# Halved roundings and squares, value tiles and group A's norm through projection banks, transposed sums, and a new first transfer order in a hybrid encoder layer

## The chip, the cores and the metric

The kernel runs on one core of one Trainium2 chip. The metric is the device time of one execution in microseconds; the time before is the median of three runs, 1087.44 us (1087.1 to 1087.69). Durations of single instructions come from one execution that the hardware profiler recorded.

The engines are called by their short names: PE is the matrix engine (PEld its weight loads), DVE the vector engine, ACT the scalar engine, POOL the general engine and SP the engine that issues most transfers. PE writes its results to eight banks of 128 x 512 floats (PSUM); DVE and ACT read them there.

## The reference, cut to what matters

One layer: an RMS norm feeds one combined projection, whose columns are split between window attention with grouped queries (group A) and neighbourhood attention on a 16 x 64 grid (group B). Each group's output gets its own RMS norm, both go through one output projection, and a gated MLP with a width-3 convolution follows. All of it is float32, 1024 tokens, model width 1024, MLP width 2816.

```python
def rmsnorm(x, g):
    y = x * lax.rsqrt(jnp.mean(x * x, axis=-1, keepdims=True) + EPS)
    return y * g

hn = rmsnorm(h, norm_mix[l])
qa, ka, va, qb, kb, vb = jnp.split(hn @ w_in[l], splits, axis=-1)
o_a = window_gqa_sink(partial_rope(qa), partial_rope(ka), va, sink[l])   # |i-j| <= 128, 8 heads, 2 kv heads
o_b = neighbourhood_attention(qb, kb, vb, rpb[l])                        # 8 x 16 window, 8 heads
mix = concatenate([rmsnorm(o_a, norm_a[l]), rmsnorm(o_b, norm_b[l])])
h = h + mix @ w_out[l]
hn = rmsnorm(h, norm_ffn[l])
h = h + (silu(conv3(hn @ w_gate[l]) + conv_b) * (hn @ w_up[l])) @ w_down[l]
return rmsnorm(h, norm_final)
```

## The kernel before

Everything is held transposed: 128 features in the partitions, 1024 tokens in the columns, so x is eight tiles of 128 x 1024. A float32 product is made of three products of rounded parts: each operand is split into a rounded high part (ACT) and the remainder (DVE), and the block `hi*hi + hi*lo + lo*hi` runs as three matmuls of 512 columns (L168 to L170, later L883 to L885). The MLP products and the down projection use sums and differences of tiles, seven products in place of eight.

**PE's order is the program's order.** `manual_schedule` pins PE; the order of the other engines is made ahead of the run from the program's order, each instruction's priority (`high_priority(offset)` lifts it) and the time at which its operands are expected. Each engine then runs its list in order.

**The head.** `load_x`, `load_first_w` issue the first transfers in a fixed order over the SP and ACT queues: x tiles by halves or whole, and the first three weight tiles in slices of the reduction dimension (`steps`). `split_x` and `split_first_w` round what has landed, in a pinned order; six accumulating products use all of it. `add_square` adds up the squares for the first norm. A transfer takes one of a few completion counters; when all are in use, the next one waits on its queue for an earlier transfer to land.

**The norms.** A sum over the features is a sum over partitions. `inverse_narrow` makes it on PE: each 128-column block of the squares is the weight, a column of ones (1/1024) the moving operand, giving 128 tokens x 1 (L199); ACT takes the square root (L202) and DVE the reciprocal (L203). `widen` turns the four columns back into a 128 x 512 row by transposing a broadcast (L210). It is called for the first norm (`vs1`), group A (`narrow_a`, `wide_a`), group B (`vb2`), the FFN norm (twice) and the final norm (half 1, then half 0 by quarters).

**Attention with a filler.** From about 60 to 380 us, PE alternates attention steps with one block at a time of the remaining projections (`rest`, jobs `Project(3)` to `Project(17)`, then `OutA(0)` to `OutA(7)`). Numbers (job, block) in `aux` say where group A's norm is placed between blocks. PSUM has four tags with two banks each: `pj` for projections, `s` for scores, `pt` for transposed probabilities, `o` for attention outputs. An attention step makes scores in `s`, DVE adds the bias and finds the maximum (L366), ACT the exponential (L370), POOL scales (L374), PE transposes into `pt` (L406 in group A, L479 in B), ACT and DVE round that (`ph` L379, `pl` L380), and PE multiplies with the values (L411, L412 and L490, L491).

After a projection, `settle` calls `post` a few blocks into the next job. For a value tile `split_v` transposes it in two halves of four 128-column blocks (L297), each into a `pt` bank, from which ACT and DVE make the rounded value and its remainder (L301, L302). For queries and keys `split_pair` or `split_qk` round 1024 columns (ACT, then DVE at L274) and send four transfers. `done` tells attention which tiles are there; `squares`, `square_b` make the squares for the norms of groups A and B, 1024 columns at a time, `normed_a` (L726) multiplies group A's output by its norm.

**The tail.** The last product of the down projection is done for half 0 of the tokens by quarters of 256 columns, two output tiles (j = 2, 3) each, 11 blocks of three matmuls per tile and quarter. `leave_quarter` adds the residual (L1283) and squares (L1328). `finish` widens the norm into two banks: DVE multiplies six tiles from one (L1309), ACT copies the other (L1303) for POOL, which multiplies the two tiles in `APART` (L1307); each tile is then stored.

Of the kernel before, what the change touches and what calls it, by code (L numbers as in the profile page):

```python
# [20 lines left out]
KT = D // 128  # L21
# [32 lines left out]
def hybrid_layer(tc, xT, w_in, w_out, w_gate, w_up, w_down, small, sink, rpb, consts, rope, out):  # L54
    nc = tc.nc
    with ExitStack() as ctx:
# [127 lines left out]
        def squares(tiles, engine):  # L184
            acc = None
            for t in tiles:
                s2 = tmp("sq")
                nc.scalar.activation(s2, t, AF.Square)
                if acc is not None:
                    engine.tensor_tensor(s2, s2, acc, op=ALU.add)  # L190
                acc = s2
            return acc

        def inverse_narrow(sqs, dim, tag, n=4):

            ps = bank("ss", tag)
            for i, sq in enumerate(sqs):
                for c in range(n):
                    nc.tensor.matmul(ps[:, c:c + 1], sq[:, c * 128:(c + 1) * 128], ones[:, 0:1], start=c == 0 and i == 0,  # L199
                                     stop=i == len(sqs) - 1, skip_group_check=True)  # L200
            v = cpool.tile([128, 4], F32, name="v4", tag="v4", bufs=4)
            nc.scalar.activation(v[:, 0:n], ps[:, 0:n], AF.Sqrt, bias=eps, scale=float(D) / dim)  # L202
            nc.vector.reciprocal(v[:, 0:n], v[:, 0:n])  # L203
            return v

# [35 lines left out]
        def split_pair(t):  # L241

            a, b = big("q", "op", F32R), big("q", "op", F32R)
            nc.scalar.activation(a, t, AF.Copy, scale=-HD ** -0.5)
            lo = t[:, :].bitcast(F32R)
            nc.vector.scalar_tensor_tensor(lo, t, -HD ** -0.5, f32(a[:, :]), op0=ALU.mult, op1=ALU.subtract)
# [22 lines left out]
        def split_qk(t):  # L269

            a, b, q = big("ka", "op", F32R), big("kb", "op", F32R), big("q", "op", F32R)
            by = cst[:, K_SCALE:K_SCALE + 1]
            nc.scalar.activation(a, t, AF.Copy, scale=by)
            nc.vector.scalar_tensor_tensor(b, t, by, f32(a[:, :]), op0=ALU.mult, op1=ALU.subtract)  # L274
# [13 lines left out]
            nc.sync.dma_start(f32(a[o:o + 64, :]), f32(b[e:e + 64, :]))  # L288
            return a, b

        def split_v(t, halves):

            v = [big("v", "op", F32R) for _ in halves]
            for g in range(2):
                ps = bank("vt", "pt")
                for c in range(4):
                    nc.tensor.transpose(ps[:, c * 128:(c + 1) * 128], t[:, (4 * g + c) * 128:(4 * g + c + 1) * 128], ident)  # L297
                for i, e in enumerate(halves):
                    src = ps[:, :].rearrange("p (c w) -> p c w", w=128)[:, :, e * 64:e * 64 + 64]
                    dst = v[i][:, :].rearrange("p (c w) -> p c w", w=128)[:, 4 * g:4 * g + 4]  # L300
                    mark["value"] = nc.scalar.activation(dst[:, :, 0:64], src, AF.Copy)  # L301
                    nc.vector.tensor_tensor(dst[:, :, 64:128], src, f32(dst[:, :, 0:64]), op=ALU.subtract)  # L302
# [208 lines left out]


        done = set()
        mg, h1, norm = [None] * 8, [None] * KT, {}

        class Project:
            def __init__(self, m):
# [28 lines left out]

            def post(self):
                post(self.m, self.t)
                done.add(self.m)

        class OutA:
            def __init__(self, d):
# [56 lines left out]
            split_first_w(m, steps[1])  # L609
        for h in range(2):  # L610
            split_x(1, tsl(h))
        for m in range(3):
            split_first_w(m, steps[2])
        acc = add_square(xts[0], None)
        for k in range(2, KT):
            split_x(k)
            if k == 3:
                for m in range(3):
                    split_first_w(m, steps[3])
# [99 lines left out]
        def wide_a():  # L719
            live["op"] += 1  # L720
            norm["a"] = big("rstda", "op")
            for h in range(2):
                nc.scalar.activation(norm["a"][:, tsl(h)], widen(norm["v"][h], "pt"), AF.Copy)

        def normed_a(i):
            return lambda: nc.vector.scalar_tensor_tensor(  # L726
                mix[i], mix[i], col(C_NA + i), norm["a"], op0=ALU.mult, op1=ALU.mult)
# [53 lines left out]
        def square_b(u):  # L781

            if u == 40:
                sums["b"] = big("sqb", "op")
                nc.scalar.activation(sums["b"], mix[4], AF.Square)
            s2 = tmp("sq")
            nc.scalar.activation(s2, mix[5 if u == 40 else 6], AF.Square)
            nc.vector.tensor_tensor(sums["b"], sums["b"], s2, op=ALU.add)

        pend = None  # L790
        for i, item in enumerate(q_until(1, 4 + AHEAD)):
# [506 lines left out]

        def finish(h, v, cols=whole, split=False):
            n = (cols.stop - cols.start) // 128  # L1300
            wide, again = widen(v, "pt", n), widen(v, "pt", n)
            copy = half("wide")
            nc.scalar.activation(copy[:, cols], again[:, 0:128 * n], AF.Copy)  # L1303
            for i, d in enumerate([d for d in range(KT) if d not in APART] + list(APART)):
                x = at_res(d, h, cols)
                if d in APART:
                    nc.gpsimd.tensor_tensor(x, x, copy[:, cols], op=ALU.mult)  # L1307
                else:
                    nc.vector.scalar_tensor_tensor(x, x, col(C_NFIN + d), wide[:, 0:128 * n], op0=ALU.mult, op1=ALU.mult)  # L1309
                (nc.scalar if split and i % 2 else nc.sync).dma_start(out[d, :, h * HALF + cols.start:h * HALF + cols.stop], x)  # L1310
# [12 lines left out]
        def leave_quarter(j, ps, cols):  # L1323
# [50 lines left out]
        for k, cols in enumerate(quarters):  # L1374
            for j in (2, 3):
                ps = banks[6, j]
                for c, (f, n) in enumerate(PARTS):
# [108 lines left out]
```

## Time and profile before

| | |
|---|---|
| time, median of three runs | 1087.44 us (1087.1 to 1087.69) |
| time of the profiled execution | 1088.62 us |
| its span, first to last instruction | 1086.8 us |
| PE busy | 1070.2 us (98%), 5144 matmuls |
| DVE busy | 860.1 us (79%), 1570 instructions |
| ACT busy | 554.5 us (51%), 1047 instructions |
| POOL busy | 105.0 us (10%) |
| moved by transfers | 144.94 MB, 133 GB/s on average |
| mean granted PE clock | 0.997 |

The profile groups instructions by the line of the program that issued them (L168), the engine, and the tiles written and read (`pj<-xgh,whi`). In the timeline a row is: start, length, engine, line, operation, out<-in, count, and in brackets how long the engine stood idle before it and what ended that. In the table of waits a row is: who waited for whom, microseconds in total, how often, the longest. Matmuls overlap in the pipeline, so a row's length is not what PE pays for it; that is the distance from one start to the next.

### The profile page before, as it was taken

What the parts mean: (1) busy time and instruction counts of PE and PEld (TensorE: products, weight loads), DVE (VectorE), ACT (ScalarE), POOL (GpSimd) and SP (SyncE); (2) the same over time, 40 slices, a digit from 0 to 9 for tenths busy, and PEclk for the clock granted to TensorE, in tenths of its full rate; (3) what the DMA queues carried; (4) which work ended last, traced back from release to release, by engine and by line L of the source; (5) the groups of instructions that cost most, each with busy time, mean ns of one, the idle gap of its engine ahead of it and who ended that gap; (6) DMA issues with size and microseconds to landing.
All of it is one profiled execution on the core that took longest, in us unless ns stands there. A gap on an engine that the chain in (4) does not pass through costs nothing.

```text
span 1086.8 us, 14983 instructions
## 1 busy us (share of the span) xinstructions
PE 1070.2 (98%) x5144; PEld 895.0 (82%) x5144; DVE 860.1 (79%) x1570; ACT 554.5 (51%) x1047; POOL 105.0 (10%) x188
## 2 busy tenths in 40 slices
PE   8999999999999999999999999999999999999997
PEld 7888888888888888887788888888888888888887
DVE  6789787667788688899998877877887867897764
ACT  7457676556676545545434334342433645444451
POOL 0223332222232100000000000000000000000001
PEclk9999999999999999999999999999999999999998
DMA  8223022232225147214342222323322788867644
GB/s 275 73 73 88 30 68 59 78 77 78 78 68 161 65 137 249 88 39 157 134 146 107 107 107 97 120 95 111 111 88 97 244 297 295 272 214 241 227 129 155
DMA packets 69084, 144.94 MB, mean 133 GB/s; under 512 B 8208, under 2 KB 19600, under 8 KB 69008
## 3 DMA queue, kind: packets, MB, share of 16 engines
q1 hardware_dynamic: 58784, 118.43, 34.6%
q10 hardware_dynamic: 10224, 25.56, 6.2%
q8 instruction: 40, 0.66, 0.3%
q14 instruction: 36, 0.29, 0.1%
HBM read 103.58 MB, written 28.57 MB: 122 GB/s over the span
## 4 chain that ended last, share of the span: by engine, by line
PE 88%; DVE 8%; ACT 2%; DMA 1%; issue 1%; SPq 0%; POOL 0%; DVEq 0%; ACTq 0%; POOLq 0%
PE pj L168 7%; PE pj L169 7%; PE pj L170 7%; PE dn L883 6%; PE dn L885 6%; PE dn L884 6%; PE z L885 5%; PE z L884 5%; PE z L883 5%; PE s L344 3%; PE x L883 3%; PE x L884 3%; PE x L885 3%; PE y L885 3%; PE y L884 3%; PE y L883 3%
## 5 line engine op out<-in xcount | busy, mean ns | idle before, releaser
L872 ACT ACTIVATE whi<-ws 128x512 fp32r<-128x512 f32 (+1 forms) x100 | 60.3, 623 | 127.8 <-DVE ws L990 80.5
L883 PE MATMUL dn<-xd,whi 128*128 128x512 f32 (+1 forms) x330 | 124.1, 376 | 0.0
L885 PE MATMUL dn<-xd,wlo 128*128 128x512 f32 (+1 forms) x330 | 123.7, 375 | 0.0
L884 PE MATMUL dn<-xd,whi 128*128 128x512 f32 (+1 forms) x330 | 123.7, 375 | 0.0
L168 PE MATMUL pj<-xgh,whi 128*128 128x512 f32 x248 | 104.4, 421 | 1.0 <-ACT xgh L584 1.0
L885 PE MATMUL z<-hg,wlo 128*128 128x512 f32 x264 | 103.0, 390 | 0.7 <-DVE wlo L873 0.7
L883 PE MATMUL z<-hg,whi 128*128 128x512 f32 x264 | 102.9, 390 | 0.0
L884 PE MATMUL z<-hg,whi 128*128 128x512 f32 x264 | 102.7, 389 | 0.0
L370 ACT ACTIVATE p<-p,nm 128x385 f32<-128x385 f32 (+3 forms) x128 | 75.1, 587 | 50.4 <-DVE nm L366 49.3
L169 PE MATMUL pj<-xgl,whi 128*128 128x512 f32 x248 | 97.5, 393 | 0.9 <-DVE xgl L585 0.8
L170 PE MATMUL pj<-xgh,wlo 128*128 128x512 f32 x248 | 97.6, 394 | 0.0
L374 POOL TENSOR_SCALAR p<-p,sm 128x384 f32<-128x384 f32 (+1 forms) x128 | 74.9, 598 | 219.3 <-DVE sm L372 204.7
L873 DVE TENSOR_TENSOR wlo<-raw,whi 128x512 fp32r<-128x512 f32 (+1 forms) x102 | 66.4, 671 | 26.6 <-ACT whi L872 26.4
L872 ACT ACTIVATE whi<-raw 128x512 fp32r<-128x512 f32 (+1 forms) x102 | 60.6, 612 | 45.2 <-DMA raw<-in_w_down_dram 20.0
L873 DVE TENSOR_TENSOR wlo<-ws,whi 128x512 fp32r<-128x512 f32 (+1 forms) x100 | 66.9, 681 | 21.0 <-ACT whi L872 20.8
L380 DVE TENSOR_TENSOR pl<-pt,ph 128x384 fp32r<-128x384 f32 (+2 forms) x108 | 63.3, 589 | 24.3 <-ACT ph L379 23.0
L1307 POOL TENSOR_TENSOR h<-h,wide 128x256 f32<-128x256 f32 (+1 forms) x6 | 5.4, 924 | 709.9 <-ACT wide L1303 709.9
L379 ACT ACTIVATE ph<-pt 128x384 fp32r<-128x384 f32 (+2 forms) x108 | 55.2, 514 | 32.2 <-PE pt L479 25.1
L885 PEld LDWEIGHTS dn<-xd,wlo 128*128 128x128 f32 x330 | 62.1, 188 | 11.3
L884 PEld LDWEIGHTS dn<-xd,whi 128*128 128x128 f32 x330 | 62.1, 188 | 11.1
L883 PEld LDWEIGHTS dn<-xd,whi 128*128 128x128 f32 x330 | 62.1, 188 | 11.1
L1198 ACT ACTIVATE xd<-xd 128x512 fp32r<-128x512 f32 x77 | 47.5, 626 | 44.0 <-DMA xd<-x 43.2
(220 smaller groups left out, 2671.2 us busy)
## 6 DMA issues: line engine op xcount, KB each, us to landing
xd<-x SPq DMA_DIRECT2D x77, 256.0 KB, 4.6
raw<-in_w_down_dram SPq DMA_DIRECT2D x72, 256.0 KB, 3.6
raw<-in_w_gate_dram SPq DMA_DIRECT2D x22, 512.0 KB, 3.4
raw<-in_w_up_dram SPq DMA_DIRECT2D x22, 512.0 KB, 3.8
x<-c ACTq DMA_DIRECT2D x22, 512.0 KB, 3.5
raw<-in_w_in_dram SPq DMA_DIRECT2D x30, 256.0 KB, 2.9
raw<-in_w_down_dram SPq DMA_DIRECT2D x36, 192.0 KB, 3.8
x<-t ACTq DMA_DIRECT2D x11, 512.0 KB, 2.6
```

The source lines that it names most:

```text
L168: nc.tensor.matmul(ps, w[0], x[0][:, tsl(h)], start=first, stop=False)
L169: nc.tensor.matmul(ps, w[0], x[1][:, tsl(h)], start=False, stop=False)
L170: nc.tensor.matmul(ps, w[1], x[0][:, tsl(h)], start=False, stop=last)
L370: nc.scalar.activation(p[:, j, 0:e], p[:, j, 0:e], AF.Exp, bias=nm, scale=-1.0, accum_out=sm[:, j:j + 1])
L374: nc.gpsimd.tensor_scalar(p[:, i, 0:m], p[:, i, 0:m], sm[:, i:i + 1], 1.0, op0=ALU.mult, op1=ALU.mult)
L379: nc.scalar.activation(ph[:, 0:n], ps[:, 0:n], AF.Copy)
L380: nc.vector.tensor_tensor(pl[:, 0:n], ps[:, 0:n], f32(ph[:, 0:n]), op=ALU.subtract)
L872: nc.scalar.activation(hi, src, AF.Copy)
L873: nc.vector.tensor_tensor(lo, src, f32(hi[:, :, :]), op=ALU.subtract)
L883: nc.tensor.matmul(ps, w[0], x[0], start=first and i == 0, stop=False, skip_group_check=True)
L884: nc.tensor.matmul(ps, w[0], x[1], start=False, stop=False, skip_group_check=True)
L885: nc.tensor.matmul(ps, w[1], x[0], start=False, stop=last and i == len(ws) - 1, skip_group_check=True)
```

## The change

The first transfers: the weights come in three slices (1, 3 and 4 of the eight blocks) in place of four, and x tile 1 goes out on ACT's queue right after x tile 0. `inverse_narrow` with one tile of squares transposes it and lets DVE add up the columns. `squares`, `split_pair`, `split_qk`, `square_b`, `normed_a` work on 512 columns at a time. A group B value tile is transposed in two steps: the first half at once and with priority into a `pj` bank, the second two blocks later into `pt`, and the tile counts as done only then. Group A's norm takes `pj` banks, one half of the tokens at a time at (12, 2), (12, 5), (12, 11) and (12, 13). `finish` widens once, and in the last stage the square of the eighth tile is added to that of the seventh before the sum; the first quarter's sum and widening come one group later.

```diff
-        steps = [slice(0, 1), slice(1, 2), slice(2, 4), slice(4, 8)]
+        steps = [slice(0, 1), slice(1, 4), slice(4, 8)]
         load_x(0, tsl(0))
         nc.scalar.dma_start(par[:, 0:C_SINK], small)
         load_x(0, tsl(1), nc.scalar)
+        load_x(1, tsl(0), nc.scalar)
+        load_x(1, tsl(1), nc.scalar)
         for m in range(3):
             load_first_w(m, steps[0])
         for m in range(3):
             load_first_w(m, steps[1])
-        load_x(1, tsl(0))
-        load_x(1, tsl(1))
-        for m in range(3):
-            load_first_w(m, steps[2])
         for k in (2, 3):
             load_x(k)
         for m in range(3):
-            load_first_w(m, steps[3])
+            load_first_w(m, steps[2])
...
             for t in tiles:
                 s2 = tmp("sq")
-                nc.scalar.activation(s2, t, AF.Square)
-                if acc is not None:
-                    engine.tensor_tensor(s2, s2, acc, op=ALU.add)
+                for h in range(2):
+                    nc.scalar.activation(s2[:, tsl(h)], t[:, tsl(h)], AF.Square)
+                    if acc is not None:
+                        engine.tensor_tensor(s2[:, tsl(h)], s2[:, tsl(h)], acc[:, tsl(h)], op=ALU.add)
...
         def inverse_narrow(sqs, dim, tag, n=4):
             ps = bank("ss", tag)
+            v = cpool.tile([128, n], F32, name="v4", tag="v4", bufs=4, padded_shape=[128, 4])
+            if len(sqs) == 1:
+                for c in range(n):
+                    nc.tensor.transpose(ps[:, c * 128:(c + 1) * 128], sqs[0][:, c * 128:(c + 1) * 128], ident)
+                nc.vector.tensor_reduce(v, ps[:, 0:n * 128].rearrange("p (c w) -> p c w", w=128), axis=mybir.AxisListType.X, op=ALU.add)
+                nc.scalar.activation(v, v, AF.Sqrt, bias=eps, scale=1.0 / dim)
+            else:
                 ...
...
         def split_qk(t):
-            nc.scalar.activation(a, t, AF.Copy, scale=by)
-            nc.vector.scalar_tensor_tensor(b, t, by, f32(a[:, :]), op0=ALU.mult, op1=ALU.subtract)
+            for h in range(2):
+                nc.scalar.activation(a[:, tsl(h)], t[:, tsl(h)], AF.Copy, scale=by)
+                nc.vector.scalar_tensor_tensor(b[:, tsl(h)], t[:, tsl(h)], by, f32(a[:, tsl(h)]), op0=ALU.mult, op1=ALU.subtract)
...
+        later = []
+        def split_v(t, halves, then=None):
...
+            if then is None:
+                group(0)
+                group(1)
+            else:
+                with tc.high_priority(offset=500):
+                    group(0, "pj")
+                later.append([2, lambda: (group(1), then())])
...
-                    vb[2 * hp], vb[2 * hp + 1] = split_v(t, (0, 1))
+                    vb[2 * hp], vb[2 * hp + 1] = split_v(t, (0, 1), lambda: done.add(m))
...
         def settle(age):
+            for item in list(later):
+                item[0] -= 1
+                if item[0] <= 0:
+                    later.remove(item)
+                    item[1]()
...
         def narrow_a():
-            norm["v"] = [inverse_narrow([norm["sq"][:, tsl(h)]], 512, "pt") for h in range(2)]
+            h = len(norm["v"])
+            with tc.high_priority(offset=500):
+                norm["v"].append(inverse_narrow([norm["sq"][:, tsl(h)]], 512, "pj"))
+        def wide_a(h):
+            def go():
+                ...
+                with tc.high_priority(offset=500):
+                    nc.scalar.activation(norm["a"][:, tsl(h)], widen(norm["v"][h], "pj"), AF.Copy)
...
-        aux[11, 8], aux[12, 6], aux[12, 12] = square_a, narrow_a, wide_a
-        for i in range(4):
-            aux[13, 3 * i + 3] = normed_a(i)
+        aux[11, 8], aux[12, 2], aux[12, 5], aux[12, 11], aux[12, 13] = square_a, narrow_a, narrow_a, wide_a(0), wide_a(1)
+        for i in range(8):
+            aux[13, 1 + i + i // 2] = normed_a(*divmod(i, 2))
...
         def finish(h, v, cols=whole, split=False):
-            wide, again = widen(v, "pt", n), widen(v, "pt", n)
+            wide = widen(v, "pt", n)
             copy = half("wide")
-            nc.scalar.activation(copy[:, cols], again[:, 0:128 * n], AF.Copy)
+            nc.scalar.activation(copy[:, cols], wide[:, 0:128 * n], AF.Copy)
...
         def leave_quarter(j, ps, cols):
             if j + NP < KT - 1:
                 nc.vector.tensor_tensor(s2, s2, sq[0][:, cols], op=ALU.add)
+            elif cols.start == 0:
+                nc.vector.tensor_tensor(s2, s2, parts[0, j - 1], op=ALU.add)
...
-                    if (k, j, c) == (1, 2, 0):
-                        vs[0] = inverse_narrow([parts[0, 2], parts[0, 3]], D, "s", 2)
                     if (k, j, c) == (1, 2, 1):
+                        vs[0] = inverse_narrow([parts[0, 3]], D, "s", 2)
+                    if (k, j, c) == (1, 3, 0):
                         finish(0, vs[0], quarters[0])
```

More of the change, by code (lines that the diff above doesn't have):

```diff
@@ L196, in inverse_narrow @@
             ps = bank("ss", tag)
-            for i, sq in enumerate(sqs):
+            v = cpool.tile([128, n], F32, name="v4", tag="v4", bufs=4, padded_shape=[128, 4])
+            if len(sqs) == 1:
                 for c in range(n):
[L199 to L202, printed above, removed]
+                    nc.tensor.transpose(ps[:, c * 128:(c + 1) * 128], sqs[0][:, c * 128:(c + 1) * 128], ident)
+                nc.vector.tensor_reduce(v, ps[:, 0:n * 128].rearrange("p (c w) -> p c w", w=128), axis=mybir.AxisListType.X, op=ALU.add)
+                nc.scalar.activation(v, v, AF.Sqrt, bias=eps, scale=1.0 / dim)
+            else:
+                for i, sq in enumerate(sqs):
+                    for c in range(n):
+                        nc.tensor.matmul(ps[:, c:c + 1], sq[:, c * 128:(c + 1) * 128], ones[:, 0:1], start=c == 0 and i == 0,
+                                         stop=i == len(sqs) - 1, skip_group_check=True)
+                nc.scalar.activation(v[:, 0:n], ps[:, 0:n], AF.Sqrt, bias=eps, scale=float(D) / dim)
             nc.vector.reciprocal(v[:, 0:n], v[:, 0:n])
@@ L243, in split_pair @@
             a, b = big("q", "op", F32R), big("q", "op", F32R)
-            nc.scalar.activation(a, t, AF.Copy, scale=-HD ** -0.5)
             lo = t[:, :].bitcast(F32R)
-            nc.vector.scalar_tensor_tensor(lo, t, -HD ** -0.5, f32(a[:, :]), op0=ALU.mult, op1=ALU.subtract)
+            for h in range(2):
+                nc.scalar.activation(a[:, tsl(h)], t[:, tsl(h)], AF.Copy, scale=-HD ** -0.5)
+                nc.vector.scalar_tensor_tensor(lo[:, tsl(h)], t[:, tsl(h)], -HD ** -0.5, f32(a[:, tsl(h)]), op0=ALU.mult, op1=ALU.subtract)
             nc.sync.dma_start(f32(b[0:64, :]), f32(a[64:128, :]))
@@ L272, in split_qk @@
             by = cst[:, K_SCALE:K_SCALE + 1]
-            nc.scalar.activation(a, t, AF.Copy, scale=by)
-            nc.vector.scalar_tensor_tensor(b, t, by, f32(a[:, :]), op0=ALU.mult, op1=ALU.subtract)
+            for h in range(2):
+                nc.scalar.activation(a[:, tsl(h)], t[:, tsl(h)], AF.Copy, scale=by)
+                nc.vector.scalar_tensor_tensor(b[:, tsl(h)], t[:, tsl(h)], by, f32(a[:, tsl(h)]), op0=ALU.mult, op1=ALU.subtract)
             nc.sync.dma_start(f32(q[0:64, :]), f32(a[0:64, :]))
@@ L289, in split_k, with group @@
             return a, b
-        def split_v(t, halves):
+        later = []
+        def split_v(t, halves, then=None):
             v = [big("v", "op", F32R) for _ in halves]
-            for g in range(2):
-                ps = bank("vt", "pt")
+            def group(g, tag="pt"):
+                ps = bank("vt", tag)
                 for c in range(4):
@@ L513, in hybrid_layer @@
         done = set()
-        mg, h1, norm = [None] * 8, [None] * KT, {}
+        mg, h1, norm = [None] * 8, [None] * KT, {"v": []}
         class Project:
@@ L548, in post @@
                 post(self.m, self.t)
-                done.add(self.m)
+                if self.m < 6 or self.m % 3:
+                    done.add(self.m)
         class OutA:
@@ L611, in hybrid_layer @@
             split_x(1, tsl(h))
-        for m in range(3):
-            split_first_w(m, steps[2])
         acc = add_square(xts[0], None)
@@ L618, in hybrid_layer @@
                 for m in range(3):
-                    split_first_w(m, steps[3])
+                    split_first_w(m, steps[2])
             acc = add_square(xts[k - 1], acc)
@@ L716, in narrow_a, with normed_a @@
         def narrow_a():
-            norm["v"] = [inverse_narrow([norm["sq"][:, tsl(h)]], 512, "pt") for h in range(2)]
[L719 to L725, printed above, removed]
+            h = len(norm["v"])
[3 more added lines that the diff above has]
+            def go():
+                if h == 0:
+                    live["op"] += 1
+                    norm["a"] = big("rstda", "op")
+                with tc.high_priority(offset=500):
+                    nc.scalar.activation(norm["a"][:, tsl(h)], widen(norm["v"][h], "pj"), AF.Copy)
+            return go
+        def normed_a(i, h):
             return lambda: nc.vector.scalar_tensor_tensor(
-                mix[i], mix[i], col(C_NA + i), norm["a"], op0=ALU.mult, op1=ALU.mult)
-        aux[11, 8], aux[12, 6], aux[12, 12] = square_a, narrow_a, wide_a
-        for i in range(4):
-            aux[13, 3 * i + 3] = normed_a(i)
+                mix[i][:, tsl(h)], mix[i][:, tsl(h)], col(C_NA + i), norm["a"][:, tsl(h)], op0=ALU.mult, op1=ALU.mult)
+        aux[11, 8], aux[12, 2], aux[12, 5], aux[12, 11], aux[12, 13] = square_a, narrow_a, narrow_a, wide_a(0), wide_a(1)
+        for i in range(8):
+            aux[13, 1 + i + i // 2] = normed_a(*divmod(i, 2))
         filler = rest()
@@ L784, in square_b @@
                 sums["b"] = big("sqb", "op")
-                nc.scalar.activation(sums["b"], mix[4], AF.Square)
+                for h in range(2):
+                    nc.scalar.activation(sums["b"][:, tsl(h)], mix[4][:, tsl(h)], AF.Square)
             s2 = tmp("sq")
-            nc.scalar.activation(s2, mix[5 if u == 40 else 6], AF.Square)
-            nc.vector.tensor_tensor(sums["b"], sums["b"], s2, op=ALU.add)
+            for h in range(2):
+                nc.scalar.activation(s2[:, tsl(h)], mix[5 if u == 40 else 6][:, tsl(h)], AF.Square)
+                nc.vector.tensor_tensor(sums["b"][:, tsl(h)], sums["b"][:, tsl(h)], s2[:, tsl(h)], op=ALU.add)
         pend = None
```

## The prediction

> **What bounds the kernel now.** I read the page first, then TensorE's waits, then the timeline where they lie.
>
> ```profile
> span 1086.8 us, 14983 instructions
> PE 1070.2 (98%) x5144; PEld 895.0 (82%) x5144; DVE 860.1 (79%) x1570; ACT 554.5 (51%) x1047; POOL 105.0 (10%) x188
> PE 88%; DVE 8%; ACT 2%; DMA 1%; issue 1%; SPq 0%; POOL 0%; DVEq 0%; ACTq 0%; POOLq 0%
> ...
> PE o L491 <- DVE pl L380: 1.4, 4, 0.6
> PE vt L297 <- DVE pl L380: 1.4, 2, 1.1
> PE pt L479 <- DVE v L302: 1.3, 1, 1.3
> ...
> PE pj L168 <- ACT xgh L584: 1.0, 1, 1.0
> PE pj L169 <- DVE xgl L585: 0.8, 1, 0.8
> PE sw L210 <- ACT rstda L723: 0.7, 1, 0.7
> ```
>
> TensorE (PE) is busy 98% of the span and is 88% of the chain of waits, so time comes from two places: instructions taken off PE's stream, and the waits that stop it. The waits are few: 1.8 us while x tile 2 is awaited (L168, L169), 1.4 + 1.3 us around the value tile (L297, L302), 0.7 us in group A's norm (L723), 1.4 us where `pl` comes late (L491). VectorE (DVE) is 79% busy: added work there hurts only where it delays something PE is about to read.
>
> **The change, part by part.** All terms are against the profiled execution, 1088.62 us (span 1086.8 and 1.82 around it). The median of the three runs, 1087.44, is 1.18 below; I take 1.18 off at the end.
>
> *Transposed sums.* Four column sums by the ones column, then four transposes of a later widening:
>
> ```profile
> 423.09 0.95 PE L199 MATMUL ss<-ones,s 128*128 128x1 f32 x8
> ...
> 423.90 0.49 PE L168 MATMUL pj<-mgh,wo 128*128 128x512 f32 x1
> ...
> 424.46 0.40 PE L170 MATMUL pj<-mgh,wo 128*128 128x512 f32 x1
> 424.69 0.40 PE L168 MATMUL pj<-mgh,wo 128*128 128x512 f32 x1
> 424.70 0.17 DVE L203 RECIPROCAL v<-v 128x4 f32<-128x4 f32 x1
> ...
> 426.76 0.60 PE L210 MATMUL sw<-cst,v 128*128 128x128 f32 x4
> 427.12 0.48 PE L168 MATMUL pj<-mgh,wo 128*128 128x512 f32 x1
> L570 DVE TENSOR_TENSOR h<-pj,xr 128x512 f32<-128x512 f32 x16 | 11.0, 687 | 3.9 <-PE pj L170 3.6
> ```
>
> From start to the start of the next product, four sums take 423.90 - 423.09 = 0.81 us (eight records for four products), four transposes 427.12 - 426.76 = 0.36. The new form is four transposes: 0.45 saved. Nine calls have one square tile and four columns (first norm 2, group A 2, group B 2, FFN norm 2, final norm's half 1): 9 x 0.45 = 4.05 us. The widening dropped in `finish` for half 1 gives 0.36 more: 4.4 together, on the path, since PE runs without a gap at these places.
>
> The price is one VectorE reduction per call, not in this trace; the nearest row is a 512-column pass that reads PSUM, 0.69 us (L570). Its cover: in the quoted place the reciprocal ends at 424.87 and its widening starts at 426.76, 1.9 us later; the reduction adds 0.69 - 0.45 = 0.24 to that path. If VectorE's queue held it 1.6 us longer, PE would stop for the excess. So 4.4, at worst 3.5.
>
> The page "TensorE: Matmul & The Clock Gate" of the Trainium skill (Part 4: PE-mode transpose) gives about 275 ns for one transpose in a kernel; if each held PE that long, four would take 1.1 us and this term would be a loss of 9 x 0.29 = 2.6 us. The rows decide: the group of four is 0.60 us long as records, but PE starts its next product after 0.36, and that is what it pays.
>
> *Value tile and group A's norm through projection banks.*
>
> ```profile
> 131.15 0.66 PE L297 MATMUL vt<-cst,t 128*128 128x128 f32 x4 [1.07 <-DVE pl L380]
> ...
> 298.28 1.28 DVE L726 SCALAR_TENSOR_TENSOR mixa<-mixa,par,rstda 128x1024 f32<-128x1024 f32 x1
> 299.95 0.75 DVE L302 TENSOR_TENSOR v<-vt,v 128x256 fp32r<-128x256 f32 x2
> 300.52 0.52 PE L479 MATMUL pt<-cst,p 128*128 128x128 f32 x3 [1.33 <-DVE v L302]
> ...
> 286.55 0.59 ACT L723 ACTIVATE rstda<-sw 128x512 f32<-128x512 f32 x1
> 287.19 0.65 PE L210 MATMUL sw<-cst,v 128*128 128x128 f32 x4 [0.69 <-ACT rstda L723]
> ```
>
> Both halves of a value tile take `pt` banks that attention's transposes also rotate through; the second half waits for `pl` (131.15), or the next attention transpose waits for the value rounding, itself behind a 1.28 us normalising pass (298.28). After the change half 0 uses the projection bank that stands empty while the other accumulates, half 1 comes two blocks later, and the normalising passes are halved. Group A's second widening no longer waits in `pt`. Of 1.4 + 1.3 + 0.7 = 3.4 us I take all 3.4: what half 1 still waits in `pt` is set against the restart of PE that each wait costs beyond its listed length. Bounds: 0, if the waits only move, and 3.4 plus about 1. A projection bank must be empty again when the next half product starts; half a product is eight blocks of three matmuls, with attention steps in between, and that is the cover (priced below).
>
> *Roundings and squares by halves.*
>
> ```profile
> L274 DVE SCALAR_TENSOR_TENSOR kb<-t,cst,ka 128x1024 fp32r<-128x1024 f32 x8 | 11.0, 1378 | 0.7 <-ACT ka L273 0.6
> L595 ACT ACTIVATE sq<-xt 128x1024 f32<-128x1024 f32 x8 | 8.4, 1049 | 0.6 <-DVE sq L597 0.6
> L1287 ACT ACTIVATE s<-h 128x512 f32<-128x512 f32 x14 | 8.8, 628 | 8.4 <-DVE h L1283 8.4
> ...
> 218.65 1.28 DVE L274 SCALAR_TENSOR_TENSOR kb<-t,cst,ka 128x1024 fp32r<-128x1024 f32 x1 [0.33 <-ACT ka L273]
> 219.93 0.87 DVE L380 TENSOR_TENSOR pl<-pt,ph 128x384 fp32r<-128x384 f32 x2
> 220.52 0.44 PE L491 MATMUL o<-pl,v 128*128 128x384 f32 x1 [0.30 <-DVE pl L380]
> ```
>
> A 1024-column pass (1.28 us) sits before the `pl` that PE needs. Halves let VectorE begin after half a rounding, so the pair ends about 0.6 us sooner; but nothing makes `pl` go between two halves, and ScalarE pays 2 x 0.63 for 1.05, about 0.2 us for each of 17 passes. Of the 1.4 us at L491 I take 0.6 (bounds -0.5 and 1.4). Splitting group A's norm into two calls three blocks apart puts exponentials between two square roots:
>
> ```profile
> 281.14 1.28 ACT L370 ACT_TABLE_LOAD   x1
> ```
>
> That is up to two more loads of 1.28 us on ScalarE, near exponentials that have about a unit of lead. I charge 0.6 (bounds 0 and 1.5).
>
> *First transfers.*
>
> ```profile
> 1.66 1.28 ACT L135 ACT_TABLE_LOAD   x1 [1.66 <-PEq L1475]
> 6.74 0.90 SPq L89 DMA_DIRECT2D xt<-in_xT_dram  x2
> 10.60 0.42 ACT L589 ACTIVATE whi<-r 128x256 fp32r<-128x256 f32 x1 [0.15 <-DMA r<-in_w_in_dram]
> 13.58 1.15 ACT L584 ACTIVATE xgh<-xt,par 128x1024 fp32r<-128x1024 f32 x1 [1.61 <-DMA xt<-in_xT_dram]
> 14.78 0.51 PE L168 MATMUL pj<-xgh,whi 128*128 128x512 f32 x1 [0.95 <-ACT xgh L584]
> 16.10 0.50 PE L169 MATMUL pj<-xgl,whi 128*128 128x512 f32 x1 [0.82 <-DVE xgl L585]
> ```
>
> x tile 2 is issued at 6.74 and lands at 13.58; its rounding and remainder stop PE. The new order has three loads fewer on SP before it, and x tile 1 goes out on ACT's queue at the start, which pushes the table load (1.66) back by two issues, some 0.9 us, and the first rounding by about 0.1. So tile 2 is issued and lands earlier, by at most about 1.5 us. Against it: the pinned order now rounds all of weight slices 1 to 3 before x tile 1. If the last of those weights lands near where the last slice-2 weights do now (10.60), tile 1's products start late and PE waits there instead; behind that wait sits the whole first projection. Taken: +0.5 (bounds -0.6 and +1.5). From tile 2 on VectorE is as tight as PE, so a gain in landing passes through both.
>
> *Tail.*
>
> ```profile
> ACT v L301 <- DVE v L302: 2.2, 4, 0.7
> ...
> 1079.94 0.88 PE L210 MATMUL sw<-cst,v 128*128 128x128 f32 x4 [0.64 <-DVE v L203]
> 1080.42 2.44 DVE L1309 SCALAR_TENSOR_TENSOR h<-h,par,sw 128x256 f32<-128x256 f32 x6 [0.63 <-PE sw L210]
> 1080.85 0.38 ACT L1303 ACTIVATE wide<-sw 128x256 f32<-128x256 f32 x1 [1.26 <-PE sw L210]
> ```
>
> Here the two widenings let VectorE multiply from one bank (1080.42) while ScalarE copies the other. With one bank they take turns: the v rows show ScalarE reading one half of a value bank only after VectorE has read the other half. The copy comes first in the program, so the six passes behind it, and the stores behind them, start 0.43 us later (0.38 and a handover). The page "PSUM — Partial Sum Buffer" of the Trainium skill (PSUM bank collisions raise a hardware error) says two engines must be kept off one bank even when both only read; the v rows agree. If the two reads did overlap, the tail would be 0.43 us better. The first quarter's sum and widening shrink from eight records to two and from four to two, some 0.75 us of PE, but its six multiplies (2.44 us) move behind one more group and end about 0.35 us after the last product could be added. 0.75 - 0.35 - 0.43: 0, bounds -0.8 and +0.4.
>
> Sum: 4.4 + 3.4 + 0.6 - 0.6 + 0.5 + 0 = 8.3 us. 1088.62 - 8.3 = 1080.3; less 1.18, **1079.1 us**.
>
> **Rivals.**
> 1. *The waits only move.* VectorE gains nine reductions (6.2 us), and two ready halves in program order act as one pass, so the change does not do what its halves promise. For it: every wait in the first table is a queue on DVE or ACT. Against: each has a named cause that goes. Only 4.4 is left: 1083.0.
> 2. *Everything goes.* All waits above vanish, and the transfers give their best: 4.4 + 3.4 + 1.4 + 1.5, and the restarts of some ten waits at 0.2: about 12.7, so 1074.7.
> 3. *The projection bank becomes the bound, slower.* Eight uses (four value halves, two sums, two widenings) borrow a bank that the next half product needs. A value half holds it for four passes that take turns, about 0.4 us each (300.52 waited 1.33 for such a bank). If PE reached it early, each use would cost 1.5 us: 12 lost against 8.3, 1091.1. It decides from 8.3 / 8 = 1.0 us a use. Against it: half a product is 24 matmuls, 0.23 us apart (424.46 to 424.69), 5.5 us, plus attention steps.
> 4. *Transposes held end to end*, at their record's length (0.27 us): 8.3 - 4.05 - 2.6 = 1.7 gained, 1085.7. The spacing in the rows above speaks against it, except where a bank is being read.
>
> **How the numbers follow.** About 0.2% (2.2 us) is what a measurement of this kernel can tell from no change. Forecast 0.55, rival 1 0.25, rival 2 0.08, rival 3 0.08, rival 4 0.04. All of the first three and little else lie below 1085.2: faster 0.86 (with a little of rival 1 lost to a bad start), same 0.06, slower 0.08. The forecast's own spread is 1076.5 to 1082.5; the range reaches to rival 1 with a late first weight, 1085.2, and to 1075.5, leaving out rival 3, most of 2 and half of 4.
>
> **What would show it.** Right: the nine sums turned into transposes of 0.36 us; no wait on vt or rstda; PE busy some 5 us less; x tile 2 rounded before 13. Wrong: PE waiting on `pj` for a value or rstda read, a wait on xgh or xgl of x tile 1, more table loads with waits behind them, or waits on `pl` as long as before.

## The result and the profile after

The changed kernel took 1090.27 us (median of ten, 1089.38 to 1092.4), the kernel before 1087.49 on the same chip: a ratio of 1.0027, interval 1.0017 to 1.0037. It is slower by about 2.8 us, where 1079.1 had been forecast. The profiled execution is 1089.86 us.

The span, the busy times and the chain of waits, from the page after:

```profile
span 1088.1 us, 14925 instructions
PE 1065.6 (98%) x5094; PEld 889.5 (82%) x5094; DVE 869.8 (80%) x1597; ACT 559.6 (51%) x1063; POOL 106.2 (10%) x188
PE 83%; DVE 9%; DMA 3%; ACT 3%; issue 1%; DVEq 0%; SPq 0%; ACTq 0%
```

TensorE's waits after (total us, number, longest):

```profile
PE sw L215 <- DVE v L208: 6.7, 4, 4.4
PE s L362 <- DMA kb<-ka: 1.8, 1, 1.8
PE o L509 <- DVE pl L398: 1.4, 2, 0.8
PE o L508 <- ACT ph L397: 1.2, 1, 1.2
```

PE is 4.6 us less busy (1070.2 before), so the work that was to leave its stream did leave. The waits around the value tile and group A's widening are gone too. In their place stand new ones: 6.7 us before widenings (`sw`, L215), 1.8 us on the transfer that completes a key tile (`kb`), 1.2 us on a rounded probability tile (`ph`). PE fell from 88% of the chain of waits to 83%.

The longest wait, 4.37 us, is in the first norm. Rows from the timelines of SP, POOL, ACT, DVE and PE after, put in order of time:

```profile
16.84 17.32 SPq L453 DMA_DIRECT2D rr<-in_rpb_dram  x3
...
30.41 0.68 DVE L159 TENSOR_TENSOR wlo<-raw,whi 128x512 fp32r<-128x512 f32 x1
...
31.90 1.71 POOL L462 TENSOR_TENSOR xb<-cst,rr 128x256 f32<-128x256 f32 x1
...
33.20 1.03 PE L199 MATMUL ss<-cst,sq 128*128 128x128 f32 x8
...
34.34 0.96 SPq L152 DMA_DIRECT2D raw<-in_w_in_dram  x2
...
38.59 0.63 ACT L158 ACTIVATE whi<-raw 128x512 fp32r<-128x512 f32 x1 [9.34 <-DMA raw<-in_w_in_dram]
39.23 1.28 ACT L201 ACT_TABLE_LOAD   x1
39.25 0.69 DVE L159 TENSOR_TENSOR wlo<-raw,whi 128x512 fp32r<-128x512 f32 x1 [5.02 <-ACT whi L158]
39.85 1.28 DVE L200 TENSOR_REDUCE v<-ss 128x4 f32<-128x512 f32 x2
40.57 0.30 ACT L201 ACTIVATE v<-v,eps 128x4 f32<-128x4 f32 x1
41.05 0.17 DVE L208 RECIPROCAL v<-v 128x4 f32<-128x4 f32 x1
...
41.37 1.78 PE L215 MATMUL sw<-cst,v 128*128 128x128 f32 x8 [4.37 <-DVE v L208]
...
42.80 0.78 PE L166 MATMUL o<-xgh,h 128*128 128x512 f32 x1
...
43.37 0.63 PE L167 MATMUL o<-xgl,h 128*128 128x512 f32 x1
43.80 0.63 PE L168 MATMUL o<-xgh,l 128*128 128x512 f32 x1
```

Read it backwards. PE waits for the reciprocal; it waits for the root, and the root for the reductions; these stand on VectorE's list behind `wlo`, the remainder of a projection weight; that needs `whi`, which ScalarE can round only at 38.59, when its weight has landed; and the load of that weight was issued at 34.34, because SP was held from 16.84 on by three loads of attention's bias (`rr`, L453). The sums had left PE at 34. Before, the same places read:

```profile
19.61 11.82 SPq L435 DMA_DIRECT2D rr<-in_rpb_dram  x2
...
31.85 0.68 DVE L161 TENSOR_TENSOR wlo<-raw,whi 128x512 fp32r<-128x512 f32 x1
...
32.55 2.14 SPq L154 DMA_DIRECT2D raw<-in_w_in_dram  x2
...
35.70 0.27 ACT L202 ACTIVATE v<-ss,eps 128x4 f32<-128x4 f32 x1 [0.63 <-PE ss L199]
35.86 0.62 ACT L160 ACTIVATE whi<-raw 128x512 fp32r<-128x512 f32 x1
```

Here two bias loads went ahead of the weights, not three, and no weight waited for them: it went out at 32.55, when VectorE's `wlo` (31.85 to 32.53) had read one of the two weight buffers and so made it free. After, a buffer was free from 31.09 (30.41 + 0.68), and the weight still stood until 34.34. A bias tile has one buffer, so each further load of it waits for GpSimd to have read the one before: the third was issued at 33.63, when GpSimd's last pass over the second had ended (31.90 + 1.71). And before, ScalarE took the root (35.70) ahead of the weight's rounding (35.86). So two orders turned over: the third bias load on SP, and root and rounding on ScalarE and VectorE.

The stretch after the wait, in the windows view (us, then busy us by engine, the granted clock, DMA share, GB/s):

```profile
41.40:45.00 3.60, 3.60 (x13) 3.20 (x14) 2.06 (x4) 1.26 (x3) 0.00 (x0) 0.53 0.12 44
```

The granted clock is 0.53: products start 0.43 us apart (43.37, 43.80) instead of 0.23. The Trainium skill's page "TensorE: Matmul & The Clock Gate" (Part 1: What's actually happening) says that TensorE falls to half its clock after an idle window of some 3.4 us and needs about as long a busy one to come back. This trace agrees: 4.4 us idle, then half clock from 41.37 to about 45.0. With the transfer order alone, below, half clock lasted longer, 5.6 us.

Three smaller losses, again from the timelines after:

```profile
276.51 1.28 ACT L201 ACT_TABLE_LOAD   x1
277.81 0.30 ACT L201 ACTIVATE v<-v,eps 128x4 f32<-128x4 f32 x1
278.12 1.28 ACT L388 ACT_TABLE_LOAD   x1
...
280.15 1.28 ACT L201 ACT_TABLE_LOAD   x1
...
281.76 1.28 ACT L388 ACT_TABLE_LOAD   x1
...
284.57 0.45 PE L508 MATMUL o<-ph,v 128*128 128x384 f32 x1 [1.24 <-ACT ph L397]
...
337.18 1.07 DVE L281 SCALAR_TENSOR_TENSOR kb<-t,cst,ka 128x512 fp32r<-128x512 f32 x1
...
339.58 0.74 DVE L281 SCALAR_TENSOR_TENSOR kb<-t,cst,ka 128x512 fp32r<-128x512 f32 x1
340.35 0.47 SPq L283 DMA_DIRECT2D q<-kb  x1
...
343.65 0.46 SPq L285 DMA_DIRECT2D kb<-ka  x1
...
349.02 0.39 PE L362 MATMUL s<-kb,q 128*128 128x256 f32 x1 [1.82 <-DMA kb<-ka]
...
424.78 0.60 PE L199 MATMUL ss<-cst,s 128*128 128x128 f32 x4
...
427.42 0.68 DVE L200 TENSOR_REDUCE v<-ss 128x4 f32<-128x512 f32 x1
...
429.54 0.62 PE L215 MATMUL sw<-cst,v 128*128 128x128 f32 x4 [1.41 <-DVE v L208]
```

Group A's two roots cost four table loads within 6.5 us, and PE then waits for `ph`. The second half of `kb` comes 2.4 us after the first, and the last transfer of the key tile, which overwrites what `q<-kb` reads, goes out 3.3 us after that one. And in the FFN norm the sums start at 424.78 and the reduction, behind VectorE's other passes, at 427.42.

### The profile page after: what moved, and what is told of

The parts are those of the page before. It is cut to its first block, busy times and chain, and to the rows that moved or that the text cites. A ratio compares the mean times of both kernels' runs of the same rounds, so it can differ in the third digit from the quotient of the medians.

```text
span 1088.1 us, 14925 instructions
## 1 busy us (share of the span) xinstructions
PE 1065.6 (98%) x5094; PEld 889.5 (82%) x5094; DVE 869.8 (80%) x1597; ACT 559.6 (51%) x1063; POOL 106.2 (10%) x188
## 4 chain that ended last, share of the span: by engine, by line
PE 83%; DVE 9%; DMA 3%; ACT 3%; issue 1%; DVEq 0%; SPq 0%; ACTq 0%
PE pj L166 6%; PE pj L168 6%; PE pj L167 6%; PE dn L914 6%; PE dn L913 6%; PE dn L912 6%; PE z L914 5%; PE z L912 5%; PE z L913 5%; PE s L362 4%; PE x L912 3%; PE x L913 3%; PE x L914 3%; PE y L914 3%; PE y L912 3%; PE y L913 3%
## 5 line engine op out<-in xcount | busy, mean ns | idle before, releaser
L913 PEld LDWEIGHTS dn<-xd,whi 128*128 128x128 f32 x330 | 62.1, 188 | 11.2
L912 PEld LDWEIGHTS dn<-xd,whi 128*128 128x128 f32 x330 | 62.1, 188 | 11.2
```

The source lines that it names most:

```text
L912: nc.tensor.matmul(ps, w[0], x[0], start=first and i == 0, stop=False, skip_group_check=True)
L913: nc.tensor.matmul(ps, w[0], x[1], start=False, stop=False, skip_group_check=True)
```

## The experiments

Two theories at first. *Queues*: the new first transfer order alone makes the first norm late. *Sums*: the reduction on VectorE's list does it. Each kernel was timed beside the kernel before, in three groups on three chips; the kernel before took 1087.63, 1087.81 and 1087.86 us there.

**Transposed sums alone.** The kernel before with the changed `inverse_narrow`:

```
+            if len(sqs) == 1:
+                for c in range(n): nc.tensor.transpose(...)
+                nc.vector.tensor_reduce(v, ...)
```

> The kernel before with one part of the change: the transposed sums (the final norm's sum keeps two tiles and so the ones column). Theory Q (queues): the first norm's stall comes from the new first transfer order, which puts three bias loads ahead of two weight loads on SP; without it VectorE's reduction has no weight remainder that waits for a transfer ahead of it. Then the sums save about 4 us of PE's stream, lose 1 to 2.5 us where VectorE holds a reduction (first norm, FFN norm), and the time is 1.5 to 3 us below before, about 1085.2. Theory S (sums): the reduction on VectorE's list is itself the cause; PE stops some 4 to 5 us in the first norm here too, and the time is 1 to 3 us above before, about 1089.5.

1086.57 us, ratio 0.9988 (0.9979 to 0.9996): faster, by 1.1 us (by 1.9 in the spans of the profiled executions). PE's wait in the first norm is here at most 0.8:

```profile
35.82 0.63 ACT L160 ACTIVATE whi<-raw 128x512 fp32r<-128x512 f32 x1 [5.80 <-DMA raw<-in_w_in_dram]
...
38.42 1.29 PE L216 MATMUL sw<-cst,v 128*128 128x128 f32 x8 [0.75 <-DVE v L209]
```

The theory *sums* falls. ScalarE rounds the weight ahead of the root here too (the roots follow at 37.77), so this order by itself came with 0.75 us of waiting; what the changed kernel adds is a weight that lands 2.8 us later (38.59 against 35.82). The gain is smaller than expected: PE's `sw` waits for reciprocals are 2.0 us, against 0.6 before.

**The new transfer order alone.** The kernel before with the changed load list and the roundings that go with it:

```
-        steps = [slice(0, 1), slice(1, 2), slice(2, 4), slice(4, 8)]
+        steps = [slice(0, 1), slice(1, 4), slice(4, 8)]
...
+        load_x(1, tsl(0), nc.scalar)
+        load_x(1, tsl(1), nc.scalar)
```

> The kernel before with one part of the change: the new first transfer order (and the order of the first roundings that goes with it). Theory Q: the first norm, still summed by the ones column, stops PE by 3.5 to 5.5 us, because the reciprocals stand behind a weight remainder that waits for a late transfer; x tile 2 gains 0.5 us; the time is 3 to 5 us above before, about 1091.5. Theory S: no stall, 0.5 us gained, about 1087.0.

1094.17 us, ratio 1.0061 (1.0049 to 1.0073): 6.5 us slower, more than expected. It is the larger effect of the two parts tried alone. Its timeline, with sums by the ones column:

```profile
17.19 17.80 SPq L433 DMA_DIRECT2D rr<-in_rpb_dram  x3
...
35.17 5.94 SPq L152 DMA_DIRECT2D raw<-in_w_in_dram  x3
...
39.40 0.63 ACT L158 ACTIVATE whi<-raw 128x512 fp32r<-128x512 f32 x1 [11.56 <-DMA raw<-in_w_in_dram]
40.05 1.28 ACT L200 ACT_TABLE_LOAD   x1
...
41.64 0.33 DVE L201 RECIPROCAL v<-v 128x4 f32<-128x4 f32 x2 [0.88 <-ACT v L200]
...
41.87 1.97 PE L208 MATMUL sw<-cst,v 128*128 128x128 f32 x8 [4.14 <-DVE v L201]
...
47.05 0.60 PE L168 MATMUL s<-xgh,w 128*128 128x512 f32 x1
47.48 0.41 PE L166 MATMUL s<-xgh,w 128*128 128x512 f32 x1
```

There is no reduction here, and the same chain: bias loads, late weight, rounding, root, reciprocal, widening. The slow products reach to 47.48. By an estimate from the starts, half clock adds some 2.7 us to the wait of 4.1: the eight transposes of the widening hold PE for 1.62 us (0.79 before), and the nine products behind them for 3.99, where 0.23 us apart they would take about 2.15.

**The old transfer order put back** into the changed kernel (the lines above in reverse):

> The changed kernel with only the first transfer order put back. Theory Q: the wait of 4.4 us in the first norm and the half-rate products behind it shrink to under 1.5 us; the time falls by 4 to 5 us to about 1085.8. Theory S: the wait stays above 3.5 us, the time within 1 us of the changed kernel's 1090.3.

1083.55 us, ratio 0.9965 (0.9955 to 0.9975): 6.7 us below the changed kernel, where 4 to 5 were expected. PE's wait in the first norm is 0.51 us. The whole loss, and more, is in the load list.

**One root for group A.** Both reductions write one tile of eight columns:

```
-                norm["v"].append(inverse_narrow([norm["sq"][:, tsl(h)]], 512, "pj"))
+                ...transposes and tensor_reduce into v8[:, 4 * h:4 * h + 4]
+                if h == 1:
+                    nc.scalar.activation(v8, v8, AF.Sqrt, ...); nc.vector.reciprocal(v8, v8)
```

> The changed kernel, but group A's two reductions go into one tile of eight columns with one square root and one reciprocal behind the second, so that two of the four table loads around 276 to 282 us go. If the loads hold the exponentials and value copies that PE awaits, the 2.2 us that PE loses at 283 to 285 us shrink below 1 and the time falls by 1.3 to 2 us, to about 1088.7. If PE waits there for something else, the time stays within 0.5 us of 1090.3.

1087.43 us, ratio 1.0002 (0.9993 to 1.001): 2.8 us below the changed kernel, more than expected. Two loads are gone, and with them PE's 1.24 us on `ph`. But the lists behind them shifted too: PE's pause before the FFN norm's widening is 0.57 us here (1.80 in the changed kernel, start to start), so not all of the 2.8 is table loads.

**Both repairs**, old order and one root:

> The changed kernel with both repairs: the first transfer order put back and group A's roots in one. If the two losses are independent, their gains add: 6.7 us (old order alone) and 2.8 us (one root alone) below the changed kernel's 1090.3, so 1080.7. If the second only moved a wait that the first stall had covered or shifted, less than 1.5 us come on top of the old order's 1083.55: above 1082.

1082.5 us, ratio 0.9959 (0.9946 to 0.9973). This is the second expectation, above 1082: 1.05 us on top of the old order, not 2.8. The interval also holds the old order alone, so by the times it is open whether anything adds; the spans of the profiled executions, 1080.1 against 1082.1, say in part.

**Only the bias loads moved.** One root for group A, the new transfer order, and:

```
+            mark["fetch"] = nc.sync.dma_start(raw, src)
...
-            nc.sync.dma_start(raw, src)
+            with behind(*["fetch"] * (h in (1, 2))): nc.sync.dma_start(raw, src)
```

> The changed kernel with group A's roots in one and its new first transfer order, and one thing moved: the second and third bias load stand behind the weight loads on SP (ACT's and VectorE's lists are unchanged). Theory Q: SP's queue, held 17 us by a bias load that waits for its single buffer, is what makes the first norm late; with the weights ahead PE's 4.4 us wait shrinks to about 1 and the half-rate products go: about 5.5 us below the one with one root alone (1087.4), 1081.9, and 0.5 us below the one with the old order (1082.5) if the new order is worth what the prediction gave it. Rival S (VectorE's list, which still has two weight remainders ahead of the reductions): the wait stays over 3 us, time above 1086.

1081.71 us, ratio 0.9945 (0.9933 to 0.9958): 5.7 us below one root alone. PE's, VectorE's and ScalarE's lists are those of one root alone, instruction by instruction, so weight rounding still stands ahead of root and reductions; it only no longer waits:

```profile
17.53 0.68 SPq L453 DMA_DIRECT2D rr<-in_rpb_dram  x1
...
29.09 4.45 SPq L152 DMA_DIRECT2D raw<-in_w_in_dram  x3
...
31.83 0.63 ACT L158 ACTIVATE whi<-raw 128x512 fp32r<-128x512 f32 x1 [3.90 <-DMA raw<-in_w_in_dram]
...
32.50 0.69 DVE L159 TENSOR_TENSOR wlo<-raw,whi 128x512 fp32r<-128x512 f32 x1 [0.86 <-ACT whi L158]
33.11 1.28 DVE L200 TENSOR_REDUCE v<-ss 128x4 f32<-128x512 f32 x2
...
36.02 1.04 PE L215 MATMUL sw<-cst,v 128*128 128x128 f32 x8
```

The weight lands 6.8 us earlier (31.83 against 38.59) and PE does not wait at all (36.02, no bracket). This settles the cause: where the bias loads stand on SP, and with it a weight that came late. Not all of the 6.8 us is the hold itself. The weight is issued 5.3 us earlier (29.09 against 34.34), and at 29.09 a buffer had just come free: VectorE's `wlo` ran from 28.32, against 30.41 in the changed kernel. So the hold itself is 34.34 - 31.09 = 3.3 us of the 5.3. The rest is VectorE running earlier: in the changed kernel two of its passes, at 24.43 and 26.40, took 2.05 and 1.75 us while GpSimd read the first bias tile, and the same two took 1.28 and 1.23 here. This share moved with the bias loads and was not tried apart. Nor are all 5.7 us the first norm: PE's wait on `kb<-ka` came out at 0.9 here and 1.9 with one root alone.

**Both repairs and the key-query pair rounded whole** (`split_qk` as before):

> The kernel with both repairs, and the rounding of a key and query pair in one pass of 1024 columns as before (halves stay everywhere else). Theory H: halving it is what delays the last transfer of the last pair (the second half of kb was queued 2.4 us behind the first on VectorE, and kb<-ka must wait until q<-kb has read its source), so PE's wait of 1.4 to 1.9 us on kb<-ka goes; at L509's place PE waits for pl again by up to 0.6 us more; net 0.8 to 1.8 us faster than with both repairs, about 1079.5. Rival: SP's queue (xr, w_out) sets that transfer, and the wait stays over 1 us; time within 0.5 us of the one with both repairs.

1080.98 us, ratio 0.9935 (0.9923 to 0.9947): 1.5 us below both repairs. PE's wait on `kb<-ka` (1.9 with both repairs) is gone. Its size is not steady, though: in the two kernels below, whose lists up to that place are those of both repairs, it is 0.8 and 1.1 us. So the halves do cause it, and their price is 0.8 to 1.9 us.

**Both repairs and all roundings and squares whole** (`split_pair`, `squares` and group B's squares too; the passes that multiply group A's output by its norm stay halved):

> The kernel with both repairs, and all roundings and squares in one pass of 1024 columns as before (split of pairs, of keys and queries, squares of both groups). If halves are worth the +0.6 us of the prediction beside the key-query pair that costs, this is slower than with only the key-query pair whole (1081.0) by 0.6 to 1 us: 1081.8. If halves do nothing but add passes, it is equal or up to 1 us faster: 1080.3.

1081.51 us, ratio 0.9943 (0.993 to 0.9955). Not to be told apart from the one above: no gain of these other halves is shown, and no loss. PE waits 2.1 us for `pl` here and 1.7 in the one above, which leans towards a small gain.

**The FFN norm's reduction ahead, or its ones column back.** Both repairs, and either a higher priority for this one sum or the old matmul sum:

```
-                    v = inverse_narrow([total[0]], D, "pt")
+                    with tc.high_priority(offset=500): v = inverse_narrow([total[0]], D, "pt")
```

> The kernel with both repairs, and the reduction of the FFN norm's half 0 put ahead on VectorE's list (higher priority for this sum alone; it then stands one to three passes earlier). If VectorE's list sets the 0.6 to 1.9 us that PE waits for the reciprocal there, they shrink below 0.4 and the time falls by 0.3 to 1.2 us below the one with both repairs. If the transposes themselves come too late, nothing changes.

> The kernel with both repairs, but the FFN norm's half 0 is summed by the ones column again. The column sum costs 0.45 us more of PE and needs no VectorE pass but the reciprocal, so PE's wait before that widening (0.6 to 1.9 us) goes: between 0.15 and 1.4 us faster than with both repairs. If this wait is due to something else than the reduction, it is 0.45 us slower.

1081.0 us, ratio 0.9942 (0.9929 to 0.9955), and 1080.99, ratio 0.9943 (0.9931 to 0.9955). In both, the pause before that widening (0.62 us with both repairs, start to start, against 0.23 without a wait) is gone, so VectorE's list set it. The 1.5 us by which the times fall are not shown to be due to it: in the profiled executions the spans are 1.1 and 0.9 us shorter, and the `kb` wait came out 1.1 and 0.8 us shorter. The two cannot be told apart: the ones column holds PE 0.45 us longer than the transposes and saves about as much waiting here.

**All repairs, with the old order and with the new.** One root, whole key-query pair, FFN sum ahead; and the same with the new order and the bias loads behind the weights:

> Old first transfer order, one root for group A, the key-query pair rounded whole, the FFN norm's half-0 reduction ahead on VectorE's list. If the last two gains (1.5 us each beside both repairs) are independent, 1079.5; if run to run they are the same effect, 1081.

> As the one with all repairs, but with the new first transfer order and the bias loads behind the weights. If the new order is worth the +0.5 us of the prediction once SP's queue is put right: 0.5 us below the one with all repairs, about 1079.0. If its later weight slices cost PE more at 6 to 12 us than x tile 2 gains: 0 to 0.6 us above it.

1080.37 us, ratio 0.9932 (0.992 to 0.9945), and 1080.51, ratio 0.9937 (0.9923 to 0.995). The first lies between its two expectations. Both beat both kernels; what the new order is worth, once SP's queue is put right, cannot be told from nothing. In the first of them PE still waits 1.7 us for `pl` and 1.6 us for reciprocals (`sw`).

## Why the prediction was wrong

**The step that failed** is the term for the first transfers, "+0.5 (bounds -0.6 and +1.5)". Alone it measured 6.5 us slower: 7.0 of the 11.2 us that lie between forecast and result. What it said of its own place held: x tile 2 was rounded early (12.12 instead of 13.58), and a first weight came a little late:

```profile
6.99 0.50 PE L166 MATMUL o<-xgh,whi 128*128 128x512 f32 x1 [0.67 <-ACT whi L608]
...
12.12 1.14 ACT L603 ACTIVATE xgh<-xt,par 128x1024 fp32r<-128x1024 f32 x1
```

But it followed SP's queue only as far as tile 2 and asked nothing of what stands behind the list that got shorter: the bias loads and the next projection's weights, issued between 15 and 37 us. Their order changed with it. Neither bound reached there, and the clock that falls after 4 us of idling was in no bound at all. In the changed kernel the weight's rounding also stands ahead of the root; that came with the transposed sums alone as well, at 0.75 us, and is dear only where the weight is late. No run keeps the three bias loads in front with the root ahead of the rounding.

**The table loads**, taken at 0.6 (bounds 0 and 1.5), were sized too small. The mechanism was named rightly, two more loads beside exponentials that have little lead. Two products at 284.57 and 285.16 start 1.63 and 0.59 us after the one before them, against 0.23 and 0.18 for such products undisturbed: 1.8 us lost. Taking the loads away gave 2.8, other shifts included (the FFN norm's pause alone is 1.2 us shorter there).

**The transposed sums** saved what they should: eight transposes from 33.20 to the next product at 33.99 are 0.79, twice the predicted 0.36 and a little. The cover did not hold: "If VectorE's queue held it 1.6 us longer, PE would stop for the excess" is what happened in the FFN norm, where sum to widening now takes 4.76 us (424.78 to 429.54; 3.67 before). Nor was it looked at anywhere but in that one place of before; alone, the sums gained 1.1 us and not 3.5 to 4.4.

**The halves** are not shown to be worth +0.6: with nearly all of them whole, the kernel with both repairs is no slower (1081.51 against 1082.5). The key-query pair's cost 0.8 to 1.9, by a path the term did not have. It looked at what VectorE does next (`pl`) and not at the four transfers behind the pair, of which the last must wait for the second. PE's wait for `pl` is 1.4 us as before.

**Value tile and group A's waits** went, as predicted, and no wait on a projection bank for a value or `rstda` read took their place: rival 3 gave the right sign by luck, since its mechanism is not there. What this part is worth in time was not tried by itself. Nor was **the tail**: the trace shows its handover, the last multiplies start 1.17 us after the start of the reciprocal instead of 0.80, 0.37 us more where 0.43 was expected; the rest of that term is not shown.

With the three repairs and the FFN sum ahead the time is 1080.37, near the 1079.1 of the forecast. This does not confirm the terms: it is another kernel, and of the 4.4 us for the sums 1.1 were found alone. The largest error was one of coverage. All bounds were drawn at the edited places; the largest loss runs through loads that the edit does not touch, and the one on `kb` ends at a transfer that it does not touch.

## What to carry to other kernels

A load list that gets shorter moves everything behind it on that queue: follow the queue on to the first transfer that waits for a buffer, and see who is behind that one. Where a new pass enters a chain on an in-order engine, look at each of its places for instructions ahead of it that wait for a transfer, not at one sample. A pass cut in halves did not help where what follows needs the whole: here the transfers of the whole tile start after the second half, and that half came 2.4 us behind the first.

## What the runs showed of the hardware

Idling has an after-price: 4.1 to 4.4 us without a product were followed by half clock for 3.7 us in the changed kernel (0.53 granted, 41.40 to 45.00) and for 5.6 us with the transfer order alone (0.50 granted, 41.87 to 47.48). Why the second lasted longer the runs do not show.

A switch of activation tables costs ScalarE 1.30 us to its next instruction (276.51 to 277.81). The Trainium skill's page "ScalarE: Activation LUTs" (What ACT_TABLE_LOAD costs) gives about 1.28 us for the load and 1.38 us of draining on top; the load agrees with the 1.28 here, and no drain shows in these rows: the activation before the load ended at 276.49, 0.02 us ahead of it.
